# Attention scores of a hybrid decoder trunk: three products over 64 rows become two products over 128 rows

## The chip, the cores and the metric

The program runs on one core of one Trainium2 chip. A core has a matrix engine (TensorE, PE in the profile, with its weight loads shown apart as PEld), a vector engine (VectorE, DVE), a scalar engine (ScalarE, ACT), a general one (GpSimd, POOL), and a queue engine that here issues nearly all transfers (SyncE, SP). Each engine works through its own list of instructions in order and waits at an instruction until what that one needs is there. Matrix products are written to PSUM, which the kernel uses as 8 banks of 128 rows by 512 floats. The metric is the device time of one execution in microseconds (us).

## The reference

All arithmetic is in 32-bit floats. The sequence has 512 tokens, the model is 1024 wide. Two layers follow one another; the first mixes with attention (16 heads of 64), the second with a short gated convolution. Each is followed by a squared-ReLU MLP and a gated embedding. The change lies in the attention:

```python
def fox_attention(h, w_in, b_f, w_out):
    proj = h @ w_in
    q, k, v = ...                                   # 16 heads of 64
    q = q * jnp.asarray(HEAD_DIM ** -0.5, q.dtype)
    log_f = jax.nn.log_sigmoid(f_logit)
    c = lax.cumsum(log_f, axis=1).transpose(0, 2, 1)
...
        s = jnp.einsum('bhqd,bhkd->bhqk', qb, k, preferred_element_type=jnp.float32)
        s = s + cb[..., :, None] - c[..., None, :]
        s = jnp.where(k_pos[None, :] <= q_pos[:, None], s, NEG_INF)
        pr = jax.nn.softmax(s, axis=-1)
        return jnp.einsum('bhqk,bhkd->bhqd', pr.astype(v.dtype), v)
```

## The kernel before

**Precision.** A product of two 32-bit matrices is made from products in a faster, rounded 32-bit type. Each operand is held as a `Pair`: `hi`, the value rounded, and `lo`, what the rounding left. `split` (L230) writes both: ACT casts to `hi`, DVE (or POOL) subtracts for `lo`. `mm3` (L222) then adds three products, hi by hi, lo by hi and hi by lo; lo by lo is left out.

**Layout.** Weights come in as 128x512 tiles (`raw`), are split into pages (`wh`, `wl`) some tiles ahead of their use (`prepare`), and 70 pages of 128x512 serve nearly everything in SBUF. PSUM tiles are taken from the 8 banks in turn as they come free.

**The attention stage.** The normed input stands transposed in `hT` (features in the rows, 512 tokens in the columns). After the values, the work goes by pairs of heads, i = 0 to 7. `project(i)` makes keys (s = 1) and queries (s = 0) of a pair: 8 steps of three products each into one bank, so 48 products of 512 columns per pair. The bank has the even head of the pair in rows 0 to 63 and the odd head in rows 64 to 127. It is written out as `kh`, `kl`, `qh`, `ql`, one page each, the queries scaled by 1/8.

`scores(i, b)` makes the scores of 128 queries (block b) against the keys up to them, for both heads of a pair, into a bank per head. A product contracts over the 64 rows of its head, `at[r, ...]` with r rows 0 to 63 or 64 to 127. For each of the three part products it issues the even head's and then the odd head's, so six products a block, of 256, 256, 384 and 512 columns for b = 0 to 3. DVE adds the forget bias and takes the maximum (L490), ACT takes the exponential and its sum (L494), POOL scales by the reciprocal (L496).

`turn(h, j)` transposes the weights of 128 keys on TensorE (bank `pT`, L503) and splits them (`ph`, `pl`); `mix(h, j)` multiplies them by the values into bank `ps_o` (L525, L526). The value pages hold hi and lo of a head beside one another in columns, so two products do here.

**What sets the order.** The main loop (L627) counts c over 64 turns. At each count it draws steps of the projection ahead (`main`, two a count, by `share + AHEAD`), then the turn of c, the mix of c - 2, and every second count the scores of a block 12 counts ahead. After the last projection the same generator gives the first products of the output projection (`o`). This order is only a priority: for most of the stage a scheduler puts the instructions in order, engine by engine, as its own model of the engines has them ready. So products of one block can end up apart from one another. The scheduler also gives out pages and banks. From two counts before the end TensorE's order is as written.

## Time and profile before

| | |
|---|---|
| median of 3 runs | 1261.39 us (1261.08 to 1261.54) |
| the profiled execution | 1261.29 us, of which the profile's span is 1259.6 us |
| PE busy in the span | 1237.6 us |
| DVE, ACT, POOL busy | 897.9, 608.5, 628.7 us |
| scores on TensorE (L484) | 192 products, the first at 81.5 us, the last at 227.2 us |

How to read it: the page of the profile gives the busy time of each engine over the whole span and, in 40 slices, its share and the clock that TensorE was granted. A view by windows gives the busy time of each engine in a stretch. A timeline lists an engine's instructions with their start and duration; durations of products overlap there, since the next one streams in while the last drains, so what a product costs is read from the step between one start and the next.

### The profile page before, as it was taken

What the parts mean: (1) busy time and instruction counts of PE and PEld (TensorE: products, weight loads), DVE (VectorE), ACT (ScalarE), POOL (GpSimd) and SP (SyncE); (2) the same over time, 40 slices, a digit from 0 to 9 for tenths busy, and PEclk for the clock granted to TensorE, in tenths of its full rate; (3) what the DMA queues carried; (4) which work ended last, traced back from release to release, by engine and by line L of the source; (5) the groups of instructions that cost most, each with busy time, mean ns of one, the idle gap of its engine ahead of it and who ended that gap; (6) DMA issues with size and microseconds to landing.
All of it is one profiled execution on the core that took longest, in us unless ns stands there. A gap on an engine that the chain in (4) does not pass through costs nothing.

```text
span 1259.6 us, 17972 instructions
## 1 busy us (share of the span) xinstructions
PE 1237.6 (98%) x6036; PEld 1021.4 (81%) x6036; DVE 897.9 (71%) x1370; ACT 608.5 (48%) x1293; POOL 628.7 (50%) x631
## 2 busy tenths in 40 slices
PE   7999999999999999999999999999999999999997
PEld 6877777788888888887889988889788888888786
DVE  5645666767788789879967444457778897779962
ACT  5445656654645434554555333244653445535541
POOL 2017555328687777876311000016777777877310
PEclk9999999999999999999999999999999999999999
DMA  7444342262432244227613233432223442245401
GB/s 254 150 140 150 102 126 76 59 226 68 134 88 90 91 134 134 82 66 236 204 34 92 76 101 101 138 130 85 93 71 105 134 126 84 69 125 168 150 18 50
DMA packets 82939, 143.43 MB, mean 114 GB/s; under 512 B 9824, under 2 KB 17040, under 8 KB 82848
## 3 DMA queue, kind: packets, MB, share of 16 engines
q1 hardware_dynamic: 82640, 142.03, 36.2%
q8 instruction: 47, 0.77, 0.3%
q14 instruction: 44, 0.36, 0.1%
q10 hardware_dynamic: 144, 0.26, 0.1%
q0 software_dynamic: 64, 0.00, 0.0%
HBM read 135.89 MB, written 6.37 MB: 113 GB/s over the span
## 4 chain that ended last, share of the span: by engine, by line
PE 81%; DVE 8%; POOL 3%; issue 3%; ACT 2%; DMA 2%; SPq 1%; DVEq 0%; POOLq 0%; ACTq 0%
PE dn L225 6%; PE up L226 6%; PE up L224 6%; PE up L225 6%; PE dn L226 6%; PE dn L224 6%; DVE wl L233 4%; PE qk L224 3%; PE qk L226 2%; PE qk L225 2%; PE sc L484 2%; PE pg L224 2%; PE pg L226 2%; PE pg L225 2%; POOL s L736 1%
## 5 line engine op out<-in xcount | busy, mean ns | idle before, releaser
L233 DVE TENSOR_TENSOR wl<-raw,wh 128x512 fp32r<-128x512 f32 (+1 forms) x372 | 345.7, 979 | 26.2 <-ACT wh L232 25.8
L225 PE MATMUL up<-hTh,wl 128*128 128x512 f32 (+1 forms) x576 | 210.2, 365 | 0.0
L226 PE MATMUL up<-hTl,wh 128*128 128x512 f32 (+1 forms) x576 | 209.7, 366 | 0.0
L224 PE MATMUL up<-hTh,wh 128*128 128x512 f32 (+1 forms) x576 | 209.4, 366 | 0.0
L232 ACT CAST wh<-raw 128x512 fp32r<-128x512 f32 (+1 forms) x372 | 201.8, 619 | 0.1
L233 POOL TENSOR_TENSOR wl<-T,wh 128x512 fp32r<-128x512 f32 x112 | 160.8, 1468 | 35.7 <-ACT wh L232 33.2
L225 PEld LDWEIGHTS up<-hTh,wl 128*128 128x128 f32 x576 | 108.6, 189 | 17.7
L224 PEld LDWEIGHTS up<-hTh,wh 128*128 128x128 f32 x576 | 108.6, 189 | 17.4
L226 PEld LDWEIGHTS up<-hTl,wh 128*128 128x128 f32 x576 | 108.3, 189 | 17.5
L768 DVE TENSOR_TENSOR acc<-dn,acc 128x512 f32<-128x512 f32 x168 | 107.5, 679 | 10.2 <-PE dn L226 10.2
L133 POOL TENSOR_TENSOR T<-raw,raw 128x512 f32<-128x512 f32 x56 | 88.1, 1585 | 37.1 <-DMA raw<-in_wdn 28.1
L722 ACT ACTIVATE r<-up 128x512 f32<-128x512 f32 (+1 forms) x72 | 38.8, 547 | 125.9 <-PE up L226 108.1
L133 POOL TENSOR_TENSOR T<-raw,T 128x512 f32<-128x512 f32 x56 | 91.8, 1639 | 2.2
L708 DVE TENSOR_TENSOR q<-r 128x512 f32<-128x512 f32 (+1 forms) x72 | 67.9, 950 | 28.7 <-ACT r L722 28.6
L247 POOL TENSOR_SCALAR cor_r_v<-cos,cos 128x1 f32<-128x1 f32 x4 | 1.6, 397 | 159.1 <-ACT junk L255 159.1
L232 ACT CAST wh<-T 128x512 fp32r<-128x512 f32 x112 | 61.2, 617 | 0.0
L232 ACT CAST A11h<-q 128x256 fp32r<-128x256 f32 x28 | 11.4, 407 | 99.9 <-DVE q L708 99.9
L224 PE MATMUL qk<-hTh,wh 128*128 128x512 f32 x128 | 52.9, 414 | 0.0
L775 POOL TENSOR_TENSOR acc<-acc,acc 128x512 f32<-128x512 f32 x28 | 46.6, 1696 | 10.4 <-DVE acc L768 10.4
L226 PE MATMUL qk<-hTl,wh 128*128 128x512 f32 x128 | 50.7, 396 | 0.0
L225 PE MATMUL qk<-hTh,wl 128*128 128x512 f32 x128 | 50.5, 395 | 0.0
L224 PE MATMUL pg<-wh,hTh 128*128 128x512 f32 x128 | 50.3, 393 | 0.0
(240 smaller groups left out, 3097.3 us busy)
## 6 DMA issues: line engine op xcount, KB each, us to landing
raw<-in_wup SPq DMA_DIRECT2D x128, 256.0 KB, 2.9
raw<-in_wdn SPq DMA_DIRECT2D x128, 256.0 KB, 2.8
raw<-in_wci SPq DMA_DIRECT2D x48, 256.0 KB, 3.5
raw<-in_wqk SPq DMA_DIRECT2D x32, 256.0 KB, 3.3
raw<-in_wpg SPq DMA_DIRECT2D x32, 256.0 KB, 3.7
g<-in_g SPq DMA_DIRECT2D x18, 256.0 KB, 6.1
prl<-neg_c SPq DMA_DIRECT2D x16, 256.0 KB, 6.7
raw<-in_wo SPq DMA_DIRECT2D x16, 256.0 KB, 2.7
```

Source lines behind the costliest of these rows:

```text
L133: nc.gpsimd.tensor_tensor(out=B[name, p], in0=B[a, p], in1=B[b, p], op=ALU.subtract)
L224: nc.tensor.matmul(ps, a.hi, b.hi, start=start, stop=False)
L225: nc.tensor.matmul(ps, a.lo, b.hi, start=False, stop=False)
L226: nc.tensor.matmul(ps, a.hi, b.lo, start=False, stop=stop)
L232: nc.scalar.copy(hi, src)
L233: eng.tensor_tensor(out=lo, in0=src, in1=hi.bitcast(F32), op=ALU.subtract)
L484: nc.tensor.matmul(ps[:, :nm], at[r, b * P : n], to[r, :nm], start=s == 0, stop=s == 2)
L708: nc.vector.tensor_tensor(out=out, in0=r, in1=r, op=ALU.mult)
L722: nc.scalar.activation(r[:, :n], ps[:, :n], AF.Relu)
L736: sums = lambda out, a, b, op: nc.gpsimd.tensor_tensor(out=out, in0=a, in1=b, op=op)
L768: nc.vector.tensor_tensor(out=a, in0=banks[s], in1=a, op=ALU.add)
L775: nc.gpsimd.tensor_tensor(out=a, in0=a, in1=acc[i, s][:, :S], op=ALU.add)
```

## The change

The pages that hold queries and keys change. Each head e of a pair now has its own page of queries, `q[e]`: the head's own 64 rows (`own[e]`) hold hi, and the other 64 rows hold lo. Each head has two pages of keys: `hi` has the head's rounded keys in both halves of the rows, `lo` has what the rounding left in the head's own rows and zeros in the other half. A product over all 128 rows of the query page with the page `hi` gives hi by hi plus lo by hi, and one with the page `lo` gives hi by lo. So a score block takes two products per head in place of three, and no step moves data by a transfer: ACT and DVE read one half of the bank and write the other half of the page.

For each pair of heads this makes 16 score products of 128 rows instead of 24 of 64; on ACT two scalings for the queries instead of one, and two casts plus two copies for the keys instead of one cast; on DVE two subtractions each for queries and keys instead of one each; on POOL two memsets of 64x512. These instructions have half the rows and the same 512 columns. A pair takes six pages instead of four. `scores` now runs through the even head's products and then the odd head's. In the main loop the projection is drawn up to six steps ahead of its share instead of two, up to its end (112 steps); the output products that follow keep their place. `stacked[i]` is set once the projection of the pair is complete.

```diff
+STACK = 6
...
-            q, key = (Pair(page(f"{n}h{i}", F32R), page(f"{n}l{i}", F32R)) for n in "qk")
-            stacked[i] = q, key
+            own = slice(0, HD), slice(HD, P)
+            q = [page(f"q{e}_{i}", F32R) for e in range(2)]
+            keys = [Pair(page(f"kh{e}_{i}", F32R), page(f"kl{e}_{i}", F32R)) for e in range(2)]
+            for e in range(2):
+                nc.gpsimd.memset(keys[e].lo[own[1 - e], :S].bitcast(F32), 0.0)
...
                 if s == 0:
-                    nc.scalar.mul(q.hi[:, :S], ps, HD**-0.5)
-                    nc.vector.scalar_tensor_tensor(
-                        out=q.lo[:, :S], in0=ps, scalar=HD**-0.5, in1=q.hi[:, :S].bitcast(F32),
-                        op0=ALU.mult, op1=ALU.subtract,
-                    )
+                    for e in range(2):
+                        hi, lo = q[e][own[e], :S], q[e][own[1 - e], :S]
+                        nc.scalar.mul(hi, ps[own[e], :], HD**-0.5)
+                        nc.vector.scalar_tensor_tensor(
+                            out=lo, in0=ps[own[e], :], scalar=HD**-0.5, in1=hi.bitcast(F32),
+                            op0=ALU.mult, op1=ALU.subtract,
+                        )
                 else:
-                    split(key.hi[:, :S], key.lo[:, :S], ps)
+                    for e in range(2):
+                        split(keys[e].hi[own[e], :S], keys[e].lo[own[e], :S], ps[own[e], :])
+                    for e in range(2):
+                        nc.scalar.copy(keys[e].hi[own[1 - e], :S], ps[own[e], :])
                 yield
+            stacked[i] = q, keys
...
-            q, key = stacked[i]
...
-            heads = [(2 * i + e, slice(64 * e, 64 * e + 64), bank(f"sc{2 * i + e}_{b}")) for e in range(2)]
-            for s, (at, to) in enumerate(((q.hi, key.hi), (q.hi, key.lo), (q.lo, key.hi))):
-                for _, r, ps in heads:
+            heads = [(2 * i + e, bank(f"sc{2 * i + e}_{b}")) for e in range(2)]
+            for (h, ps), at, key in zip(heads, *stacked[i]):
+                for s, to in enumerate((key.hi, key.lo)):
                     nc.tensor.matmul(
-                        ps[:, :nm], at[r, b * P : n], to[r, :nm], start=s == 0, stop=s == 2
+                        ps[:, :nm], at[:, b * P : n], to[:, :nm], start=s == 0, stop=s == 1
                     )
...
-            while done < share + AHEAD:
+            while done < max(share + AHEAD, min(share + STACK, 112)):
```

The scheduler makes a new order of it. The first place is TensorE at the block b = 2 of the pair i = 4 (`sc_2`, 384 columns; `qk` is a projection of a later pair, `ps_o` a mix, `pT` a turn). Before:

```order
L225 MATMUL qk_0_2142<-hTh,wl_1461 128x512
L484 MATMUL sc_2_2176<-kh_1686,qh_1684 128x384
L484 MATMUL sc_2_2176<-kl_1687,qh_1684 128x384
L484 MATMUL sc_2_2176<-kh_1686,ql_1685 128x384
L226 MATMUL qk_0_2142<-hTl,wh_1460 128x512
L224 MATMUL qk_0_2142<-hTh,wh_1460 128x512
L225 MATMUL qk_0_2142<-hTh,wl_1461 128x512
L226 MATMUL qk_0_2142<-hTl,wh_1460 128x512
L224 MATMUL qk_0_2142<-hTh,wh_1504 128x512
L484 MATMUL sc_2_2177<-kh_1686,qh_1684 128x384
L484 MATMUL sc_2_2177<-kl_1687,qh_1684 128x384
L525 MATMUL ps_o_2117<-ph_2_2113,v_1_141 128x256
```

The same block of the same pair after the change:

```order
L512 MATMUL pT_0_2203<-ident,prl_1527 128x128
L493 MATMUL sc_2_2214<-kh_4_1658,q_4_1656 128x384
L493 MATMUL sc_2_2214<-kl_4_1659,q_4_1656 128x384
L534 MATMUL ps_o_2154<-ph_2_2150,v_1_141 128x256
L493 MATMUL sc_2_2215<-kh_4_1660,q_4_1657 128x384
L493 MATMUL sc_2_2215<-kl_4_1661,q_4_1657 128x384
L535 MATMUL ps_o_2154<-pl_2_2151,v_1_141 128x256
L225 MATMUL qk_1_2260<-hTh,wh_1665 128x512
```

Before, the two heads' products of this block stood five projection products apart, and the odd head's were cut once more by a mix. Now one mix stands between the heads, and the projection behind them is that of the next pair but one.

The second place is ACT where the keys of the pair i = 5 are split (`kh`; `ph` are casts of turned weights, `pr` exponentials). Before:

```order
L494 ACTIVATE pr_1781,sm_1_2129<-pr_1781,nmx_1_2128 128x256
L232 CAST kh_1982<-qk_1_1984 128x512
L232 CAST ph_2_2113<-pT_2_2110 128x256
L494 ACTIVATE pr_1781,sm_1_2136<-pr_1781,nmx_1_2135 128x256
L232 CAST ph_3_2151<-pT_3_2149 128x128
L232 CAST ph_0_2170<-pT_0_2165 128x512
```

After:

```order
L233 CAST kh_5_1956<-qk_1_1962 64x512
L503 ACTIVATE prl_1638,sm_3_2025<-prl_1638,nmx_3_2024 128x512
L233 CAST kh_5_1958<-qk_1_1962 64x512
L233 CAST ph_0_2076<-pT_0_2071 128x512
L503 ACTIVATE prr_1826,sm_0_2089<-prr_1826,nmx_0_2088 128x128
L463 CAST kh_5_1956<-qk_1_1962 64x512
L463 CAST kh_5_1958<-qk_1_1962 64x512
L233 CAST ph_1_2113<-pT_1_2109 128x384
```

Where one cast of a key bank stood, four instructions stand among the casts of turned weights and the exponentials, the last two directly ahead of the cast `ph_1`.

The third place is TensorE after the change, from block b = 1 to block b = 2 of the pair i = 2, with what each instruction waits for (`sc_1_1562` is the odd head's block 1; the even head's stands right ahead of it):

```order
L493 MATMUL sc_1_1562<-kh_2_1149,q_2_1146 128x256 [waits DVE_49]
L493 MATMUL sc_1_1562<-kl_2_1150,q_2_1146 128x256
L512 MATMUL pT_3_1587<-ident,prl_706 128x128 [waits Activation_49]
L534 MATMUL ps_o_1558<-ph_1_1517,v_0_136 128x384 [waits Activation_49]
L535 MATMUL ps_o_1558<-pl_1_1518,v_0_136 128x384 [waits DVE_49]
L512 MATMUL pT_0_1607<-ident,prr_1048 128x128 [waits PE_49]
L512 MATMUL pT_0_1607<-ident,pr_1046 128x128
L512 MATMUL pT_0_1607<-ident,prr_1048 128x128
L512 MATMUL pT_0_1607<-ident,prl_1047 128x128 [waits Pool_49]
L493 MATMUL sc_2_1618<-kh_2_1147,q_2_1145 128x384 [waits DVE_49]
L493 MATMUL sc_2_1618<-kl_2_1148,q_2_1145 128x384
L493 MATMUL sc_2_1619<-kh_2_1149,q_2_1146 128x384 [waits DVE_49]
```

The odd head's block 2 (last row) goes into the bank of the even head's block 1 and waits until DVE has read that; before the change blocks 1 and 2 of a pair had a turn, a mix and eleven projection products between them.

More of the change, by code (lines that the diff above doesn't have):

```diff
@@ L475, in scores @@
         def scores(i, b):
-            q, key = stacked[i]
             n = (b + 1) * P
             nm = max(n, 256)
-            heads = [(2 * i + e, slice(64 * e, 64 * e + 64), bank(f"sc{2 * i + e}_{b}")) for e in range(2)]
-            for s, (at, to) in enumerate(((q.hi, key.hi), (q.hi, key.lo), (q.lo, key.hi))):
-                for _, r, ps in heads:
+            heads = [(2 * i + e, bank(f"sc{2 * i + e}_{b}")) for e in range(2)]
+            for (h, ps), at, key in zip(heads, *stacked[i]):
+                for s, to in enumerate((key.hi, key.lo)):
                     nc.tensor.matmul(
-                        ps[:, :nm], at[r, b * P : n], to[r, :nm], start=s == 0, stop=s == 2
+                        ps[:, :nm], at[:, b * P : n], to[:, :nm], start=s == 0, stop=s == 1
                     )
-            for h, _, ps in heads:
+            for h, ps in heads:
                 pr = probs[h][b]
```

## The prediction

> **What bounds the kernel now.** I read the page first, for the engine that has no room, then windows of the attention stage, then TensorE's timeline in it.
>
> ```profile
> span 1259.6 us, 17972 instructions
> PE 1237.6 (98%) x6036; PEld 1021.4 (81%) x6036; DVE 897.9 (71%) x1370; ACT 608.5 (48%) x1293; POOL 628.7 (50%) x631
> PE   7999999999999999999999999999999999999997
> PEclk9999999999999999999999999999999999999999
> 127.39:148.07 20.68, 20.68 (x110) 15.32 (x110) 13.43 (x41) 12.55 (x33) 11.00 (x21) 1.00 0.42 115
> 148.07:168.75 20.68, 20.68 (x110) 15.32 (x110) 13.38 (x41) 12.50 (x33) 11.65 (x22) 1.00 0.37 116
> 227.60:250.00 22.40, 21.62 (x113) 17.25 (x114) 16.86 (x38) 15.24 (x36) 6.67 (x11) 1.00 0.21 60
> ```
>
> TensorE is busy in 98% of the span at the full granted clock. The columns of the window rows are the length, then busy time of PE, weight loads, DVE, ACT and POOL, the clock, and the transfers' share and GB/s. One pair of heads takes 20.68 us in the middle of the attention stage, the same in both rows, and TensorE has no idle time in it. DVE and ACT are busy 13.4 and 12.5 us. So a product that goes, or gets shorter, shortens the stage, as long as the others keep up. After the last scores (third row) TensorE idles 0.8 us of 22.4.
>
> **What a score block costs TensorE.** Prices are steps between starts on TensorE's timeline. The first two rows are the first and the last of 24 back-to-back products of 512 columns; the last two of the next group, the first and the last of 15 of 256.
>
> ```profile
> 76.01 0.39 PE L224 MATMUL qk<-hTh,wh 128*128 128x512 f32 x1
> 81.22 0.39 PE L226 MATMUL qk<-hTl,wh 128*128 128x512 f32 x1
> ...
> 159.85 0.34 PE L525 MATMUL ps_o<-ph,v 128*128 128x384 f32 x1
> 160.03 0.40 PE L224 MATMUL qk<-hTh,wh 128*128 128x512 f32 x1
> ...
> 161.81 0.27 PE L503 MATMUL pT<-ident,pr 128*128 128x128 f32 x1
> 161.92 0.27 PE L503 MATMUL pT<-ident,prr 128*128 128x128 f32 x1
> ...
> 299.74 0.28 PE L225 MATMUL up<-hTh,wl 128*128 128x256 f32 x1
> 301.42 0.28 PE L224 MATMUL up<-hTh,wh 128*128 128x256 f32 x1
> ```
>
> 512 columns: (81.22 - 76.01) / 23 = 0.2265 us. 384: 0.18 at most; I take 0.175. 256: 1.68 / 14 = 0.12. A transpose: 0.11. All are products over 128 rows, each with its own weights.
>
> Now the score blocks of 64 rows in the same stretch:
>
> ```profile
> 157.46 0.40 PE L526 MATMUL ps_o<-pl,v 128*128 128x512 f32 x1
> 157.79 0.39 PE L484 MATMUL sc<-kh,qh 64*128 64x256 f32 x2
> ...
> 158.68 0.40 PE L225 MATMUL qk<-hTh,wl 128*128 128x512 f32 x1
> ...
> 162.37 0.40 PE L225 MATMUL qk<-hTh,wl 128*128 128x512 f32 x1
> 162.69 0.44 PE L484 MATMUL sc<-kh,qh 64*128 64x384 f32 x1
> ...
> 163.76 0.40 PE L224 MATMUL qk<-hTh,wh 128*128 128x512 f32 x1
> ...
> 164.46 0.40 PE L224 MATMUL qk<-hTh,wh 128*128 128x512 f32 x1
> 164.79 0.44 PE L484 MATMUL sc<-kh,qh 64*128 64x384 f32 x1
> ...
> 165.33 0.39 PE L525 MATMUL ps_o<-ph,v 128*128 128x256 f32 x1
> 165.65 0.43 PE L484 MATMUL sc<-kh,ql 64*128 64x384 f32 x1
> 166.01 0.33 PE L503 MATMUL pT<-ident,pr 128*128 128x128 f32 x1
> ...
> 168.35 0.40 PE L526 MATMUL ps_o<-pl,v 128*128 128x512 f32 x1
> 168.68 0.50 PE L484 MATMUL sc<-kh,qh 64*128 64x512 f32 x2
> ...
> 169.92 0.40 PE L225 MATMUL qk<-hTh,wl 128*128 128x512 f32 x1
> ```
>
> "x2" means that the two heads' products start within the same instant: two products of 64 rows share the array. But the array loses time on entering and on leaving this form: the step from the 512-column product at 157.46 to the first score is 0.33 instead of 0.23, and again 0.34 before 158.68. A block of 256 together with both turns costs 158.68 - 157.46 less two products of 512, so 1.22 - 0.45 = 0.77 us. The block of 512 costs 1.57 - 0.45 = 1.12. The block of 384 is split by the order: the heads are apart, nothing runs beside anything, and the turns are paid again: 1.39 - 0.45 = 0.94 for the one head, 1.55 - 0.23 - 0.12 = 1.20 for the other. A pair has two blocks of 256: 0.77 + 0.77 + 2.14 + 1.12 = **4.8 us**.
>
> From the other side: what of the 20.68 us is not scores? 48 projection products (10.87), 20 transposes (2.2), and for each head two mixes of 512, 384, 256 and 256 columns (4 x 0.6415 = 2.57) make 15.64, which leaves **5.04** for scores and every small wait.
>
> After the change a block is four products over 128 rows without a change of form: 4 x (0.12 + 0.12 + 0.175 + 0.2265) = **2.57 us** for a pair, wherever the order puts them. So TensorE gets 2.2 to 2.47 us per pair, times 8 pairs 17.8 to 19.8 us. The first pairs split less and the last ones split more than the middle ones; I take **18.5**.
>
> The sharing of the array speaks against the change, and there is a rule for it. The Trainium skill (TensorEngine Tiling (Array Packing), "Theoretical Speedup" and "Key Properties") gives up to twice the rate where the contraction is 64 or less, and says that changing the tiling mode drains the engine. By the first rule alone the old pair would cost 6 x 0.6415 / 2 = 1.92 us; the trace has 4.8, and it agrees with the second rule.
>
> **What the new splits cost elsewhere.** Nothing of this is on TensorE. The first row is the page's; the others are of the window 148.07 to 168.75 by line and form, then two lines of the whole run.
>
> ```profile
> L233 DVE TENSOR_TENSOR wl<-raw,wh 128x512 fp32r<-128x512 f32 (+1 forms) x372 | 345.7, 979 | 26.2 <-ACT wh L232 25.8
> ...
> L448 ACT ACTIVATE qh<-qk 128x512 fp32r<-128x512 f32 x2 | 1.2, 600 | 0.0
> L530 ACT COPY o<-ps_o 64x512 f32<-64x512 f32 x2 | 1.2, 582 | 0.0
> L233 DVE TENSOR_TENSOR kl<-qk,kh 128x512 fp32r<-128x512 f32 x1 | 0.7, 691 | 0.1
> L531 DVE TENSOR_TENSOR oT<-ps_o,o 64x512 f32<-64x512 f32 x3 | 2.1, 691 | 0.9 <-ACT o L530 0.9
> L225 PEld LDWEIGHTS qk<-hTh,wl 128*128 128x128 f32 x16 | 3.0, 188 | 0.3
> L606 POOL MEMSET ones<- x1: 526/526/526, 21.2 to 21.2; 128x512 f32 x1
> L510 POOL MEMSET ph<- x16: 197/208/210, 109.6 to 236.4; 128x128 f32 x16
> ```
>
> An ACT copy of 64x512 that crosses the halves of the rows takes 0.58 (L530), a DVE subtraction of 64x512 0.69 (L531); the rows of 128x512 beside them (L448, L233) take 0.60 and 0.69, so half the rows save nothing. A subtraction that writes the other half isn't in the trace; the page's mean for L233 over all forms is 0.98, which I take as its upper bound, and 0.69 as its value. ACT gets four more instructions a pair, 2.3 us: 12.5 + 2.3 = 14.8 of a pair time of 20.68 - 2.3 = 18.4. DVE gets two, 1.4 us (2.0 at most): 14.8 to 15.4 of 18.4. POOL gets two memsets of 64x512, between 0.21 (L510) and 0.53 (L606) each: at most 12.7 of 18.4. So all three still fit under TensorE, ACT and DVE at 80% instead of 60 to 65%, and TensorE's work is the cover. Behind a memset on POOL stand the scalings of weights (L496), which turns need some counts later; a memset waits for a page only.
>
> What is late next is a bank or a split. In the third piece of the order, the odd head's block 2 waits for the read of the even head's block 1. From the start of that head's last product TensorE has 3 x 0.12 + 0.11 + 2 x 0.175 + 4 x 0.11 + 2 x 0.175 = 1.6 us until then. How long the read takes, the timeline shows:
>
> ```profile
> 178.81 0.28 PE L484 MATMUL sc<-kh,ql 64*128 64x256 f32 x2
> ...
> 179.13 0.42 DVE L490 CUSTOM_DVE_ANT_0 pr<-sc,pr 128x256 f32<-128x256 f32 x1 [0.79 <-PE sc L484]
> ```
>
> It starts 0.32 after the last products do and takes 0.42: 0.74. With one subtraction of 0.69 ahead of it on DVE that is 1.4, just enough; with two it is 0.5 short. I count four pairs with this place. Likewise the cast `ph_1` now stands behind two key copies. I allow **2 us** in all for such waits, with 0 and 10 as ends. The first scores are covered: 24 projection products (5.4 us) lie between the end of the first queries and the first score, and the query split now takes 2 x (0.58 + 0.69) = 2.5 us. After the attention both orders are the same, and the rest of the program moves forward as a whole.
>
> A new price could also be wrong. If a weight load (0.19) weren't hidden behind a product of 256 columns, each of the 64 such products would cost 0.07 more, 4.5 us; the row of 15 such products at 0.12 speaks against it.
>
> **Sum.** 1261.29 us for the profiled execution (its span 1259.6 and 1.7 around it; 0.1 under the median of 1261.39) - 18.5 + 2 = 1244.8, so **1245 us**.
>
> **Rivals.**
> - *Evictions come late in every pair.* TensorE waits 1.2 us a pair for banks and for `ph`, since ACT and DVE have 3.6 us a pair left where they had 7 to 8. 8 x 1.2 = 9.6 instead of 2: 1252.4. For it: the tight bank and the copies ahead of `ph_1`. Against it: today's steady pairs have no such wait.
> - *The end has less cover.* The projection is drawn four steps earlier, so 12 products, 2.7 us, are gone from the last pairs, where TensorE already idles (0.8 us in the third window). All of it lost: 1247.5.
> - *Weight loads show:* 1249.3, as above.
> - *Slower: ACT sets the pace.* The four extra instructions and the two subtractions stand in front of the casts and exponentials that TensorE's next mix and turn need, and their 2.3 + 1.4 = 3.7 us a pair go onto its path. Above 2.3 us of wait a pair the gain is gone; 3.7 makes the pair 1.4 longer, and with 8 pairs 1261.3 + 11 = 1272. Against it: 3.6 us of slack, and mixes two counts (about 4.6 us) behind their turns.
> - *Slower: the pairing was worth more.* If the two heads shared the array at full rate and the 4.8 us were waits that the new order has too, the pair would go from 1.92 to 2.57, +0.65 x 8: 1266.5. The first rule of the Trainium skill's page from above would have it so. The rows of a lone head at 384 columns, 0.94 for three products, speak against it.
> - *It doesn't do what it says:* no fewer score products. The order shows four a block; only a stage bound by something else would leave the time as it is, 1261.
>
> **Chances.** Forecast 0.62, late evictions 0.14, the end 0.10, weight loads 0.04, no change 0.03, ACT 0.05, pairing 0.02. The likeliest one's own range is 1241 to 1247; with the next three on the upper side, and 18.5 going to 19.8 with no wait on the lower, 1240 to 1255 holds about 8 in 10. About 0.2%, 2.5 us, is what a measurement can tell here: faster 0.90, same 0.03, slower 0.07.
>
> **What would show it.** Right: windows of 18.3 to 18.7 us for a middle pair with PE still busy throughout, score products in steps of 0.12 to 0.23, ACT near 14.8 and DVE near 14.8 in it. Late evictions: idle time of PE before `sc` or `ps_o` that ends on DVE or ACT, with windows near 19.5. The end: more idle time after the last scores than 0.8. It would be wrong outright if TensorE's idle time in the stage passed 18 us, or if the stage after the attention gave the gain back.

## The result, and the profile after

The changed kernel takes **1249.2 us** (median of 4 runs, 1248.1 to 1250.8) where the kernel before took 1261.4 beside it: a ratio of 0.990, with an interval of 0.989 to 0.992. The profiled execution took 1249.03 us. The forecast was 1245 with a range of 1240 to 1255; of the 16.3 us that it saw as gain, 12.2 came.

The page of the profile after the change, its span and its busy times:

```profile
span 1247.3 us, 17921 instructions
PE 1222.8 (98%) x5972; PEld 1024.7 (82%) x5972; DVE 909.4 (73%) x1386; ACT 626.1 (50%) x1325; POOL 639.4 (51%) x647
```

TensorE is busy 14.8 us less and is still the engine that bounds the kernel, at 98%. DVE, ACT and POOL each do 11 to 18 us more.

Windows of the attention stage after the change (length, then busy time of PE, weight loads, DVE, ACT, POOL, then the clock, the transfers' share and GB/s), and from TensorE's timeline three times the same transpose, in three neighbouring pairs of heads:

```profile
110.00:128.00 18.00, 18.00 (x101) 15.49 (x99) 14.35 (x42) 14.41 (x36) 15.05 (x28) 1.00 0.45 129
128.00:147.00 19.00, 19.00 (x105) 16.33 (x104) 15.37 (x45) 15.19 (x38) 12.58 (x21) 1.00 0.42 126
184.00:220.00 36.00, 34.07 (x179) 27.39 (x178) 29.49 (x89) 28.38 (x74) 21.74 (x33) 0.95 0.30 74
```

```profile
128.96 0.27 PE L512 MATMUL pT<-ident,pr 128*128 128x128 f32 x1
...
147.32 0.27 PE L512 MATMUL pT<-ident,pr 128*128 128x128 f32 x1
...
165.72 0.27 PE L512 MATMUL pT<-ident,pr 128*128 128x128 f32 x1
```

A pair now takes 147.32 - 128.96 = 18.36 and 165.72 - 147.32 = 18.40 us, where it took 20.68. In the middle of the stage (first two windows) TensorE has no idle time, with DVE and ACT busy 14.4 to 15.4 us of 18 to 19. The third window, where the attention ends, has 1.9 us of idle time and a clock of 0.95 instead of 1.00. So the pairs came as forecast, and what is missing is missing at the end of the stage.

The rows of the score products, before and after (their durations, then the first and the last start):

```profile
L484 PE MATMUL sc<-kh,ql x64: 271/307/435, 81.9 to 227.2; 64*128 64x256 f32 x32, 64*128 64x384 f32 x16, 64*128 64x512 f32 x16
```

```profile
L493 PE MATMUL sc<-kl,q x64: 279/308/628, 81.6 to 214.5; 128*128 128x256 f32 x32, 128*128 128x384 f32 x16, 128*128 128x512 f32 x16
```

They begin within 0.3 us of the same time and end 12.7 us earlier; the rest of the program follows as a whole.

**Where the missing part went.** To see it I went over all of TensorE's steps from the first score to the last, a step being the time from one start to the next. "Score steps" are those at the score products and at the one product before and behind them, less the price of what in them is no score (0.2265, 0.172, 0.12 and 0.11 us for 512, 384, 256 and 128 columns). "Other over price" is what all other steps take above their prices. The end of the scores is the point where their last step ends, the start of the second product behind the last score. All times in us; the experiments of the next section are in the table already.

| kernel | profiled execution | end of the scores | score steps | other over price |
|---|---|---|---|---|
| before | 1261.29 | 227.8 | 38.5 | 1.6 |
| **the change** | 1249.03 | 214.9 | 21.2 | 5.9 |
| the change again | 1248.09 | 213.2 | 20.6 | 4.9 |
| the change, lead of 2 | 1252.52 | 217.5 | 22.2 | 7.4 |
| before, lead of 6 | 1261.76 | 227.7 | 38.6 | 1.4 |
| before, the split work alone | 1267.17 | 234.1 | 46.9 | -0.1 |
| before, heads in turn | 1264.17 | 231.2 | 43.0 | 0.5 |
| the change, 12 idle products in the gap | 1249.09 | 214.6 | 21.1 | 2.1 |
| the change, bound at 118 | 1246.83 | 212.0 | 21.3 | 3.2 |
| the same again | 1246.44 | 212.5 | 21.2 | 3.2 |
| the change, bound at 113 | 1246.85 | 211.6 | 20.6 | 2.7 |
| the change, lead taken back late | 1250.86 | 214.2 | 21.2 | 5.3 |
| the change, key copies on POOL | 1254.50 | 219.8 | 28.0 | 4.0 |
| the change, no key copies | 1245.80 | 211.6 | 20.5 | 3.4 |

The score steps fell by 17.2 us (before rounding). The other steps rose by 5.9 - 1.6 = 4.3 us, and nearly all of that lies in one place. The view of waits over the whole stretch from 81 to 215 us lists three waits of TensorE's products, and TensorE's timeline has them together:

```profile
PE ps_o L534 <- ACT ph L233: 1.6, 2, 1.1
PE ps_o L534 <- POOL ph L519: 0.2, 1, 0.2
```

```profile
195.50 0.39 PE L534 MATMUL ps_o<-ph,v 128*128 128x256 f32 x1 [0.54 <-ACT ph L233]
...
196.72 0.39 PE L534 MATMUL ps_o<-ph,v 128*128 128x256 f32 x1 [0.18 <-POOL ph L519]
...
198.31 0.50 PE L534 MATMUL ps_o<-ph,v 128*128 128x512 f32 x1 [1.06 <-ACT ph L233]
```

1.78 us of idle time. Held against their prices, the steps from the last transpose ahead of the first wait (194.69) to 198.31 take 2.8 us too much: 3.62 us for 0.81 us of products. ACT's timeline says what the last cast `ph` stood behind:

```profile
195.50 0.60 ACT L454 ACTIVATE q<-qk 64x512 fp32r<-64x512 f32 x1
...
197.05 0.59 ACT L454 ACTIVATE q<-qk 64x512 fp32r<-64x512 f32 x1 [0.36 <-DVE q L455]
197.67 0.59 ACT L233 CAST ph<-pT 128x512 fp32r<-128x512 f32 x1
```

The two halves of the last query split stand ahead of the cast, the second one waiting for DVE to finish its part of the first. This is the moment at which the last projection is done. In the order the projection, drawn six steps ahead, has reached its bound of 112 steps at count 40, and at the counts 41 and 42 nothing is drawn; behind the last `qk` TensorE has only turns, mixes and scores up to the first output product, each of which needs something from ACT, DVE or POOL, and shortly before and in the gap ACT and DVE have the last keys, the last queries and the first splits for the output to do.

Right behind the gap the clock falls. Windows of the profiled execution of the result, and then of another execution of the same kernel ("the change again" in the table):

```profile
198.00:200.00 2.00, 1.69 (x6) 1.37 (x7) 1.83 (x5) 1.95 (x6) 1.42 (x2) 0.78 0.10 34
200.00:202.00 2.00, 2.00 (x6) 1.61 (x5) 1.94 (x6) 1.58 (x4) 1.78 (x7) 0.50 0.00 0
202.00:204.00 2.00, 2.00 (x9) 1.55 (x8) 1.25 (x4) 0.82 (x2) 1.86 (x2) 0.87 0.00 0
```

```profile
198.00:200.00 2.00, 1.71 (x7) 1.42 (x8) 1.82 (x5) 1.95 (x6) 1.41 (x2) 1.00 0.00 0
200.00:202.00 2.00, 2.00 (x10) 1.67 (x9) 1.94 (x6) 1.57 (x4) 1.77 (x7) 1.00 0.00 0
202.00:204.00 2.00, 2.00 (x12) 1.66 (x12) 1.24 (x4) 0.92 (x3) 1.86 (x2) 1.00 0.00 0
```

TensorE looks busy in both, but the rows count 21 products in the first and 29 in the second. The clock of the first three rows takes away 2 x (0.22 + 0.50 + 0.13) = 1.7 us of full clock; the scores end 214.9 - 213.2 = 1.6 us apart. Eight steps fall into the half clock, and three of them count as score steps: the last two of the block of 512 columns behind the gap and the product after it, which take 1.27 us instead of 0.68. So 0.6 us of the clock is in the 21.2 us of score steps (20.6 in the second execution, at full clock), and 1.0 in the other steps. The account of the result is: 1261.3 - 17.9 (score steps at full clock, 38.5 to 20.6) + 1.6 (half clock) + 2.8 (gap) + 0.5 (other steps) + 0.6 (the rest of the program, 1031.8 us before and 1032.4 after) = 1248.9.

### The profile page after: what moved, and what is told of

It is laid out like the page before. It is cut to its first block, busy times and chain, and to the rows that moved or that the text cites. A ratio compares the mean times of both kernels' runs of the same rounds, so it can differ in the third digit from the quotient of the medians.

```text
span 1247.3 us, 17921 instructions
## 1 busy us (share of the span) xinstructions
PE 1222.8 (98%) x5972; PEld 1024.7 (82%) x5972; DVE 909.4 (73%) x1386; ACT 626.1 (50%) x1325; POOL 639.4 (51%) x647
## 4 chain that ended last, share of the span: by engine, by line
PE 74%; DVE 10%; POOL 5%; issue 4%; ACT 3%; DMA 3%; SPq 0%; DVEq 0%; POOLq 0%; ACTq 0%
PE dn L226 6%; PE dn L227 5%; PE up L226 5%; PE up L225 5%; PE up L227 5%; PE dn L225 5%; DVE wl L234 5%; POOL s L745 3%; PE pg L227 2%; PE pg L225 2%; PE pg L226 2%; PE qk L225 2%; PE qk L226 2%; PE qk L227 2%; DVE acc L777 2%
## 5 line engine op out<-in xcount | busy, mean ns | idle before, releaser
L233 ACT CAST A11h<-q 128x256 fp32r<-128x256 f32 x28 | 11.4, 406 | 100.7 <-DVE q L717 100.7
L784 POOL TENSOR_TENSOR acc<-acc,acc 128x512 f32<-128x512 f32 x28 | 46.9, 1707 | 10.0 <-DVE acc L777 10.0
```

Of the source, the lines that this page charges most:

```text
L233: nc.scalar.copy(hi, src)
L784: nc.gpsimd.tensor_tensor(out=a, in0=a, in1=acc[i, s][:, :S], op=ALU.add)
```

## The experiments

Beside each kernel the kernel before was run on the same chip; ratios are to it.

### The lead of the projection, without and alone

The change with the projection drawn two steps ahead, as before:

```diff
-STACK = 6
+STACK = 2
```

> The changed kernel with the projection drawn two steps ahead instead of six (STACK = 2); everything else as changed. Theory (the hole after the last projection, 2.4 us of idle TensorE, and the half clock after it, 1.9 us, come from drawing the projection early): five to seven projection products stand in the hole again, no half clock, and with the steady pairs as they are 1245 to 1246 us. Rival (the splits need the six steps): the queries and keys come too late for the scores, TensorE waits about 0.5 us or more in every pair, 1250 us or more.

Measured: 1254.3 us (1252.5 to 1258.2), ratio 0.9945 (0.9932 to 0.9959), so 5 us slower than the change. The 1245 to 1246 us of the theory did not come. The time is the rival's, though the waits stand at a few places, not in every pair. A window of this kernel and its largest wait up to 215 us:

```profile
122.00:130.00 8.00, 5.41 (x27) 4.08 (x26) 6.56 (x16) 6.76 (x16) 4.29 (x9) 1.00 0.28 98
```

```profile
PE ps_o L534 <- ACT ph L233: 1.8, 1, 1.8
```

Without the lead the waits come inside the stage: 2.6 us of idle time in one window of 8. The end, on the other hand, has projection products left and no gap. So in the changed kernel the lead buys the cover in the middle with the one at the end.

The other side of it, the kernel before with the lead:

```diff
+STACK = 6
...
-            while done < share + AHEAD:
+            while done < max(share + AHEAD, min(share + STACK, 112)):
```

> The kernel before, its products and splits unchanged, with the projection drawn six steps ahead. Theory (the gain is the products', the early projection only opens the hole): between 1260 and 1265 us, with an idle stretch of 2 us or more and a half clock near the end of the attention; what is lost there may be made up in part by pairs that stay together. Rival (a good part of the gain is the new order): 1255 us or less.

Measured: 1261.9 us (1261.4 to 1264.4), ratio 1.0004 (0.9995 to 1.0013). Score steps and other steps stay within 0.2 us. By itself the lead is worth nothing: the old splits needed no cover. But the idle stretch and the half clock that I expected near the end did not come either: the view of waits lists none of TensorE's products from 82 to 230 us, and the clock is 1.00 there. From the last projection product to the first output product (207.44 to 211.64 us) this kernel takes 4.2 us, for 27 turns, mixes and scores in between that are worth 4.3 us one by one. The changed kernel takes 8.3 us in its second execution, at full clock, for 31 worth 4.7. So the lead alone does not open the gap. It takes the lead together with something else of the change, the split work on ACT and DVE or the order; which of them was not separated.

### The split work without the products

The kernel before, with its six products a block of 64 rows, but with the split work of the change: scalings, casts and subtractions per head, two more copies, two memsets, two more pages a pair.

```diff
+            spare = [page(f"kx{e}_{i}", F32R) for e in range(2)]
+            for e in range(2):
+                nc.gpsimd.memset(spare[e][own[1 - e], :S].bitcast(F32), 0.0)
...
+                    for e in range(2):
+                        split(key.hi[own[e], :S], key.lo[own[e], :S], ps[own[e], :])
+                    for e in range(2):
+                        nc.scalar.copy(spare[e][own[e], :S], ps[own[e], :])
```

> The kernel before with its six products a block, but with the changed kernel's work on ACT, DVE and POOL: queries and keys are split by halves, two copies and two memsets a pair go to a page that nothing reads. Theory (this work hides under TensorE): 1261 to 1263 us, ACT busy about 14.8 us in a middle pair. Rival (ACT sets the pace): 1264 us or more, with TensorE idle in every pair.

Measured: 1268.0 us (1267.2 to 1268.5), ratio 1.0050 (1.0036 to 1.0063). It is slower, and not by any wait: the steps outside the scores are at their prices (-0.1 us in all), and in a window of the middle TensorE has no idle time:

```profile
128.00:147.00 19.00, 19.00 (x96) 13.98 (x95) 13.90 (x38) 13.03 (x33) 9.95 (x18) 1.00 0.35 112
```

What rose are the score steps, from 38.5 to 46.9 us. TensorE's timeline shows how:

```profile
138.03 0.39 PE L226 MATMUL qk<-hTl,wh 128*128 128x512 f32 x1
...
138.40 0.48 PE L534 MATMUL ps_o<-ph,v 128*128 128x512 f32 x1
138.81 0.39 PE L493 MATMUL sc<-kh,qh 64*128 64x256 f32 x1
139.04 0.28 PE L493 MATMUL sc<-kl,qh 64*128 64x256 f32 x1
139.16 0.28 PE L493 MATMUL sc<-kh,ql 64*128 64x256 f32 x1
139.37 0.50 PE L535 MATMUL ps_o<-pl,v 128*128 128x512 f32 x1
139.80 0.38 PE L493 MATMUL sc<-kh,qh 64*128 64x256 f32 x1
```

With other work on ACT and DVE the scheduler made another order, and in it a mix stands between the heads of a block. Each head takes 139.37 - 138.40 - 0.2265 = 0.74 us by itself, nearly as much as both of them took together before the change (0.77). So this run doesn't price the split work in the old kernel, as it was meant to. It shows something else: the cost of the old score products hung on the order that the scheduler happened to find. The products over 128 rows don't have this: 20.5 to 22.2 us in all orders of the table but one, where they wait for banks.

### The pairing of the two heads

The kernel before, with the odd head's three products issued behind the even head's, to take the sharing of the array away:

```diff
-            for s, (at, to) in enumerate(((q.hi, key.hi), (q.hi, key.lo), (q.lo, key.hi))):
-                for _, r, ps in heads:
+            for _, r, ps in heads:
+                for s, (at, to) in enumerate(((q.hi, key.hi), (q.hi, key.lo), (q.lo, key.hi))):
```

> The kernel before with the odd head's three products issued after the even head's, so that no two products of 64 rows stand side by side. By the rows of before: a block of 256 goes from 0.77 to 0.92 us, one of 512 from 1.12 to 1.56, the split one stays, so +0.75 us a pair, 1266 to 1268 us. If pairing gave the full double rate: 1275 us or more. If it gave nothing: 1261 us.

Measured: 1264.4 us (1263.9 to 1264.8), ratio 1.0021 (1.0012 to 1.0029). But the edit didn't take the sharing away. In the kernel's list of instructions for TensorE a block now reads

```
L484 MATMUL sc_0_2326<-kh_1982,qh_1980 128x256
L484 MATMUL sc_0_2326<-kl_1983,qh_1980 128x256
L484 MATMUL sc_0_2326<-kh_1982,ql_1981 128x256
L484 MATMUL sc_0_2327<-kh_1982,qh_1980 128x256
L484 MATMUL sc_0_2327<-kl_1983,qh_1980 128x256
L484 MATMUL sc_0_2327<-kh_1982,ql_1981 128x256
```

(the first three of the even head, the others of the odd), and a block of this form on the timeline:

```profile
132.94 0.39 PE L484 MATMUL sc<-kh,qh 64*128 64x256 f32 x2
133.17 0.29 PE L484 MATMUL sc<-kl,qh 64*128 64x256 f32 x2
133.28 0.29 PE L484 MATMUL sc<-kh,ql 64*128 64x256 f32 x2
```

Still two at a time: the fourth product of the list starts with the first. (The count "x2" alone only says that the view has merged two like instructions; their starts in the trace are 132.944 and 132.954 us.) So what a kernel without the pairing would take was not measured. What can be read is how the score steps come about, by three counts from the timelines: the products at their prices one after another, what is saved where two start together (within 0.03 us), and what is left, the turns, over the number of unbroken groups.

| kernel | one after another | pairs that start together | saved by them | groups | left, for a group |
|---|---|---|---|---|---|
| before | 30.8 | 66 of 96 | 10.0 | 45 | 17.6, 0.39 |
| before, lead of 6 | 30.8 | 68 | 11.4 | 48 | 19.1, 0.40 |
| before, heads in turn | 30.8 | 60 | 9.3 | 51 | 21.5, 0.42 |
| before, the split work alone | 30.8 | 48 | 8.0 | 57 | 24.1, 0.42 |

(30.8 is 8 x 6 x 0.6415.) Every group pays about 0.4 us for its two changes of form, whatever stands in it: in the kernel before, 27 of the 45 groups share no neighbouring product with another group, and 26 of these pay 0.39 to 0.43 us each, those of three products as much as those of six and the one of twelve. (The last group, at 226.42 us, pays 0.21.) This gives the change's gain a plainer form than the prediction had: a third of the products less is worth 30.8 - 20.5 = 10.3 us, the lost pairing costs 10.0, and the turns, 17.6, are all gone; 0.7 of the new score steps is above their price, 0.6 of it the half clock. 10.3 - 10.0 + 17.6 - 0.7 = 17.2. By this count the gain is as large as the turns.

### The gap: filling it with nothing, with work, and moving it

Twelve products of 512 columns that nobody reads, put into the gap (two counts with six each):

```diff
+            if c in (41, 42):
+                ps = bank(f"fill{c}")
+                for m in range(6):
+                    nc.tensor.matmul(
+                        ps, vs[m % 4][0][:, :P], vs[m % 4][1][:, :S], start=m == 0, stop=m == 5
+                    )
```

> The changed kernel with 12 further products of 512 columns in two spare banks, drawn at counts 41 and 42, whose results nothing reads; they read value pages only. It is more work, 2.7 us, in the place where TensorE idled 2.4 us. Theory (the idle stretch makes the clock drop to a half, which costs another 1.9 us): no half clock, a mean clock of 0.998 or more in all runs, and 1247 to 1248 us in spite of the added work. Rival (the drop has another cause): half clock as before and 1249.5 to 1252 us.

Measured: 1249.5 us (1248.7 to 1251.6), ratio 0.9906 (0.9893 to 0.9920), the same as the change. 12 x 0.2265 = 2.7 us of work came in nearly for nothing: from the first score to the last this execution takes 0.4 us longer than the change again, and the other steps fell from 4.9 to 2.1 us over price, by the 2.8 of the gap. The clock behind the place stays at 1.00. That the time would also fall to 1247 to 1248 us, because the clock stays up, did not come true; the runs' mean clocks are 0.996 to 0.998, not 0.998 or more, and the profiled execution had half the clock at another place, from 17 to 20.5 us, so that its scores begin 0.9 us later than the change's.

The same with real work. The bound on the lead is raised by six steps, so that the first output products are drawn into the gap:

```diff
-            while done < max(share + AHEAD, min(share + STACK, 112)):
+            while done < max(share + AHEAD, min(share + STACK, 118)):
```

> The changed kernel with the cap of 112 steps raised to 118, so that the first steps of the output projection are drawn right behind the last projection and stand in the hole (24 products). Theory (the hole only lacks cover): no half clock there, 2.4 + 1.9 us less and about 1 us of new waits later, where these products then lack: 1245.5 to 1247 us. Rival (the cover only moves, the hole opens further on): 1249 us or more.

Measured: 1246.6 us (1246.0 to 1248.9), ratio 0.9884 (0.9869 to 0.9900). Then the change, this kernel, and one with the bound at 113 were run side by side:

> The change once more, unaltered, so that the next three stand beside it on the same chip. Theory: 1248.0 to 1250.8 us as in its first four runs. If the half clock behind the gap at 195 to 198 us comes in some executions and not in others, its runs spread by about 1.7 us, while those of the two kernels without the gap lie closer together.

> The change with the bound at 118 steps once more. Theory: 1246.0 to 1247.5, about 2.5 us under the change on the same chip. Rival (the first comparison caught a lucky set of runs): within 1 us of the change.

> The change with the bound of the lead at 113 steps instead of 112: the first output products come one step earlier, 12 of them into the gap behind the last projection and 12 more after the next block of 512 columns. Theory (the gap of 1.8 us and the half clock behind it were the whole difference between forecast and result): 1245.0 to 1247.0, as with 118, because 12 products (2.7 us) are enough to cover both. Rival (those 12 products are missing later, where the last scores wait): 1248 to 1250, the gap only moves to 200 to 212 us.

Measured: the change 1248.9 us (1248.1 to 1249.9), ratio 0.9902 (0.9889 to 0.9916); 118 steps 1246.4 (1245.9 to 1247.6), ratio 0.9883 (0.9870 to 0.9897); 113 steps 1246.6 (1245.5 to 1251.3), ratio 0.9889 (0.9872 to 0.9905). Windows of the kernel with 118:

```profile
196.00:198.00 2.00, 2.00 (x11) 1.63 (x10) 1.91 (x7) 1.62 (x5) 2.00 (x8) 1.00 0.53 94
198.00:200.00 2.00, 2.00 (x10) 1.68 (x9) 1.30 (x3) 1.00 (x3) 1.41 (x2) 1.00 0.23 68
```

No idle time where the gap was. A part of the loss has moved: one wait of 0.5 us comes at 205 us, and all steps from 200 to 210 us together are 1.8 us over price, where the change again has 0.1 there and the kernel with 113 steps 0.6. 2.5 us of the medians are won in this comparison; the first comparison of both, from separate runs, gives 1249.2 - 1246.6 = 2.6. The runs of the change and of 118 steps don't overlap here, though the intervals of their ratios touch. By the medians one step more is as good as six: the 12 products of that step are what the gap needs. What I expected of the spread was wrong: the kernel with 113 has no gap and the widest runs of the three. Their mean clocks go from 0.999 in one of the fastest to 0.994 in the slowest; its profiled execution has a piece of half clock from 16.8 to 20.2 us, far ahead of the scores.

Then an attempt to leave the gap out by giving up the lead late in the stage, from count 34 on:

```diff
-            while done < max(share + AHEAD, min(share + STACK, 112)):
+            while done < max(share + AHEAD, min(share + (STACK if c < 34 else AHEAD), 112)):
```

> The changed kernel with six steps of lead until count 33 and two from count 34 on: the steady pairs keep their lead, the last projection is stretched over the hole as before the change. Theory (both belong together: the lead for the steady pairs, the cover for the end): 1244.5 to 1247 us, no half clock. Rival (the last pair needs the lead too): its queries come late, idle time ahead of the last pair's scores, 1249 us or more.

Measured: 1250.6 us (1247.3 to 1251.5), ratio 0.9908 (0.9894 to 0.9921): nothing gained. The time is in the rival's range, but the wait stands before a mix, not before the scores. The gap is there still, with another releaser and its largest wait in one piece; from the view of waits:

```profile
PE ps_o L534 <- POOL ph L519: 2.6, 1, 2.6
```

### The added work on ACT

The copies of the rounded keys into the other half of the rows, made by POOL:

```diff
-                        nc.scalar.copy(keys[e].hi[own[1 - e], :S], ps[own[e], :])
+                        nc.gpsimd.tensor_copy(keys[e].hi[own[1 - e], :S], keys[e].hi[own[e], :S])
```

> The changed kernel with the two copies of the rounded keys into the other half made by POOL from the page, not by ACT from the bank: 1.2 us a pair less on ACT, more on POOL. If the late casts of turned weights in the hole come from ACT's pile-up: part of the 2.4 us of idle and with luck the half clock go, 1246 to 1248 us. If only the missing products count: 1248.5 to 1250 us. If the slower copy makes the keys late: 1251 us or more.

Measured: 1254.6 us (1253.6 to 1255.1), ratio 0.9943 (0.9931 to 0.9956), 5 us slower than the change. The view of TensorE's waits lists those before score products, and the timeline has one of them:

```profile
PE sc L493 <- DVE nmx L499: 1.3, 3, 0.5
```

```profile
129.47 0.28 PE L493 MATMUL sc<-kl,q 128*128 128x256 f32 x1
130.19 0.39 PE L493 MATMUL sc<-kh,q 128*128 128x256 f32 x1 [0.43 <-DVE nmx L499]
```

Three such waits of 0.43 to 0.46 us: the odd head's block waits until the maximum of an earlier block has been read from the bank. The first score of 512 columns in a pair starts at 146.99, 166.53 and 186.07 us, so a middle pair takes 19.5 us, where the change takes 18.4. The score steps, 28.0 us, have the larger part of this; only some of it is idle time in the views. This is close to the rival of late evictions in every pair, which had 19.5, in a kernel where it holds. The gap behind the last projection is here too: 1.9 us of waits, with half the clock behind it. The copy takes 0.61 us on POOL (median) and 0.58 on ACT, so its own time isn't the reason; why DVE is late here, whether by the order that came of it or by POOL's scalings, was not settled.

Last, no copies at all. POOL writes zeros in their place, so the part of the scores that is `lo` of the queries by `hi` of the keys is left out; the products are the same in number and form.

```diff
+                nc.gpsimd.memset(keys[e].hi[own[1 - e], :S].bitcast(F32), 0.0)
...
-                    for e in range(2):
-                        nc.scalar.copy(keys[e].hi[own[1 - e], :S], ps[own[e], :])
```

> The change without the two copies of rounded keys per pair that ACT makes; POOL writes zeros there instead, so the part lo by hi of the scores is left out. Products on TensorE are the same in number and form. Theory (in the middle pairs the added ACT work is hidden under TensorE, and it shows only in the gap behind the last projection): 1247.0 to 1249.0, ACT 1.2 us less busy in a middle pair, which stays at 18.4 to 18.6 us, and the gap is smaller by up to 1.2 us. Rival (the copies hold up casts in every pair): 8 times 0.6 to 1.2 us less, 1240 to 1245.

Measured: 1246.2 us (1245.8 to 1246.5), ratio 0.9880 (0.9867 to 0.9894), 2.7 us less than the change beside it. A window in the middle of the stage, and the gap:

```profile
128.00:147.00 19.00, 19.00 (x104) 16.39 (x103) 14.90 (x42) 13.64 (x36) 13.70 (x25) 1.00 0.41 126
```

```profile
196.08 0.51 PE L533 MATMUL ps_o<-ph,v 128*128 128x512 f32 x1 [1.13 <-ACT ph L233]
```

ACT has 1.5 us less to do in the window, and TensorE is as busy as with the copies: in the middle they are hidden. Of three waits in the gap one is left, 1.13 us instead of 1.78 in all, and the scores end 213.2 - 211.6 = 1.6 us earlier than in the change again. The median is under the range I had set by 0.8 us and far from 8 pairs with 0.6 to 1.2 us each. Of the 1.6 us, 1.5 are in the other steps (4.9 to 3.4: the gap, less a new wait at 207 us) and 0.2 in the score steps; the rest of the 2.7 lies behind the scores and in the spread of the runs, which I did not follow up.

## Why the prediction was right, and where it was off

- **TensorE bounds the stage, so shorter products shorten it.** Right. A pair went from 20.68 to 18.36 and 18.40 us; 18.3 to 18.7 was said.
- **The score products, 18.5 us.** The mechanism was right, the size 0.6 too large: 38.5 - 20.6 = 17.9 at full clock, and 17.2 with the half clock that fell on three of the steps. The new products take 20.6 / 8 = 2.58 us a pair, 2.57 was said. The old ones took 38.5 / 8 = 4.81 us; the rows of the blocks had given 4.8. The other way of working it out, 5.04 from what is left of a pair, had small waits in it which stay after the change, and I leaned toward it.
- **The price of the new splits.** Right: the rows of the changed kernel are

```profile
L463 ACT CAST kh<-qk x16: 577/582/587, 73.4 to 191.0; 64x512 fp32r<-64x512 f32 x16
L455 DVE SCALAR_TENSOR_TENSOR q<-qk,q x16: 683/688/696, 76.8 to 197.7; 64x512 fp32r<-64x512 f32 x16
L441 POOL MEMSET kl<- x16: 517/520/523, 65.7 to 180.5; 64x512 f32 x16
```

  0.58, 0.69 and 0.52 us, where 0.58, 0.69 and at most 0.53 were taken. A copy or subtraction that writes the other half of the rows (0.58 and 0.69) costs no more than one that stays in its half (`kh` and `kl` of the same kernel, 0.58 and 0.69).
- **They are covered by TensorE.** Right in the pairs, as the run without copies shows: 1.5 us less on ACT in 19, and nothing more from TensorE.
- **The allowance of 2 us for waits.** This is the term that was mis-sized: 4.9 us came. It was also put in the wrong place. It was worked out for the odd head's block 2 in four pairs, behind the read of the even head's block 1, and for `ph_1` behind the key copies; in the changed kernel's stage TensorE's products have none of these waits. (The kernel before had fourteen projection products between blocks 1 and 2 of that pair, not eleven, which changes nothing here.) What came is one gap behind the last projection, 2.8 us, the half clock behind the gap, 1.6 us, which no step of the prediction held, and 0.5 us of small steps. That the result still lies in the range is owed to the wide upper end of this term, not to its reasons: that part is luck.
- **The rest of the program.** "The rest moves forward as a whole" was right to 0.6 us.
- **The rival "the end has less cover".** It comes nearest to what happened: the projection is drawn four steps earlier, and those 12 products, 2.7 us, are missing at the end. The 12 idle products that cost 0.4 us and the 2.3 to 2.5 us won by drawing 12 output products earlier fit this size. But it was not the whole mechanism: in the kernel before the same lead left no gap. Its sign in the profile was wrong, too: more idle time *after* the last scores was said, and the gap lies before them, at 195 to 198 us. I had looked at the end of the stage where TensorE idled already, not at the point where the projection runs out. The order of the changed kernel shows that place without a run: from the last `qk` to the first `o` no product that is free of ACT, DVE and POOL.
- **The rival "weight loads show".** Its number, 1249.3, is almost the measured one, but its mechanism is not there. The products of 256 columns go in steps of 0.12 us in the changed kernel, as before:

```profile
192.20 0.28 PE L493 MATMUL sc<-kh,q 128*128 128x256 f32 x1
192.32 0.28 PE L493 MATMUL sc<-kl,q 128*128 128x256 f32 x1
```

- **The rival "evictions come late in every pair".** The pairs of 18.4 us without idle time rule it out for the changed kernel; it came in the kernel with the copies on POOL.
- **The slower rivals.** ACT doesn't set the pace in the pairs. "The pairing was worth more" was half true: two products of 64 rows do share the array at the full rate where nothing breaks them. In the block quoted with the heads in turn, two products of 256 columns go in one step of 133.28 - 133.17 = 0.11 us. The first rule of the Trainium skill (TensorEngine Tiling (Array Packing), "Theoretical Speedup"), up to twice the rate, agrees with this for the 66 of 96 pairs that start together. What the rival needed besides was that the rest of the 4.8 us is waits that stay. It is turns, and they went: some 0.4 us a group by the counts above. The other rule of the Trainium skill, that a change of tiling mode drains the engine (the same page, "Key Properties"), agrees with that; it gives no price.

## What to carry to other kernels

Where an engine's work moves ahead, look at the point where it runs out: the cover that it gave is missing there. The order shows the place before any run, but not whether the engine will idle at it: with the lead alone it did not. Products of 64 rows among products of 128 paid a fixed price for each unbroken group (0.4 us here), so count the groups in the order, not the products; under a scheduler another edit may add to them (from 45 to 57 here, with 18 fewer pairs that start together, 8 us). Where an edit brought 12 us of a forecast of 16, going over the steps of the bounding engine against their prices found most of the rest in one place, and output work drawn ahead of it (118 or 113 steps instead of 112) won back 2.3 to 2.5 us.

## What the runs showed of the hardware

**The clock falls to half in pieces of 3.41 us, and the same kernel with the same gap may or may not have one.** The result's profiled execution had it from 199.1 to 202.5 us behind 1.78 us of idle time in three waits, the longest 1.06; the second execution had the same three waits to within 0.02 us and kept 1.00. In the records of the clock of all 14 traces each stretch between two changes is a whole multiple of 3.413 us: in the result's execution 184.32 us at full clock (54 times), 3.41 at half, then 1041.07 (305 times). So the clock changes on a grid, and the grid begins at another point in each execution. Windows laid on it, first the result's, then the second execution's, then two places of the kernel that gave up the lead late:

```profile
195.68:199.10 3.42, 2.18 (x9) 1.39 (x10) 3.29 (x11) 3.04 (x8) 3.10 (x8) 1.00 0.33 103
199.10:202.51 3.41, 3.41 (x10) 2.64 (x8) 3.21 (x11) 2.56 (x7) 2.93 (x7) 0.50 0.02 6
...
196.88:200.30 3.42, 2.36 (x11) 1.82 (x12) 3.18 (x9) 3.11 (x7) 2.83 (x5) 1.00 0.07 25
200.30:203.71 3.41, 3.41 (x18) 2.81 (x16) 2.87 (x9) 2.16 (x5) 3.04 (x8) 1.00 0.00 0
...
196.89:200.31 3.42, 1.72 (x10) 1.51 (x11) 0.45 (x3) 1.87 (x6) 3.11 (x7) 1.00 0.33 116
200.31:203.72 3.41, 3.41 (x17) 2.86 (x16) 3.32 (x9) 2.91 (x7) 2.34 (x4) 1.00 0.00 0
...
582.60:586.02 3.42, 1.59 (x7) 0.99 (x7) 3.31 (x6) 2.82 (x5) 0.00 (x0) 1.00 0.90 291
586.02:589.43 3.41, 3.41 (x10) 2.63 (x9) 3.28 (x6) 0.93 (x2) 0.00 (x0) 0.50 0.73 259
```

The half clock came behind a window with 1.24 us of idle time and behind one with 1.83, and not behind those with 1.06 and 1.70 (there the grid cut one wait of 2.57 us in two). Where the grid cuts a gap fits the difference between the two executions of the change. Idle time in a window is not the whole rule, since 1.70 did less than 1.24; what else counts was not tested. The Trainium skill (TensorE: Matmul & The Clock Gate, "What's actually happening") describes a free-running activity window of 3413 ns and half the clock after an idle one. The length of the pieces and the moving grid agree with that, but none of the windows here was idle throughout. The advice of the Trainium skill (the same page, "Why this matters for your kernels") to keep gaps under some 3 us was not enough here: the half clock came behind three waits of at most 1.06 us each, and behind one of 1.83.

**Two products on different halves of the rows start together even where the kernel's list has three of the one ahead of the other's first**, within 0.01 us (132.944 and 132.954 us in the kernel with the heads in turn). So the order in the list alone doesn't say whether two heads share the array. What puts them side by side, the engine or a step between the list and the chip, is not shown.

**Work on half the rows costs about the same as on all of them** on ACT and DVE (0.58 and 0.69 us for 64x512; 0.60 and 0.69 for 128x512 in the rows of the prediction), so a split that is made in two halves takes about twice the time of one over all rows.
